# First plain tile closed early, and casts ahead of low parts where a gated MLP's blocks begin: a float32 trunk on one Trainium2 core

## The chip, the cores and the metric

The kernel runs on one core of one Trainium2 chip, as one program. The metric is the time of one execution on the device in microseconds (us). The times of before are the median of three runs, and one further execution was profiled. The engines are called as the profile calls them: PE is TensorE (PEld its weight loads), DVE is VectorE, ACT is ScalarE, POOL is GpSimd, and SP is SyncE, which only issues transfers here.

## The reference

A two-layer encoder trunk over 512 tokens of width 1024, in float32. Layer 0 mixes by a matrix memory (mLSTM), layer 1 by chunked band attention, and both read a memory of 256 tokens by cross attention. What matters here is the channel mixer that closes each layer:

```python
def causal_dwconv(x, w, b):              # width 3 here
    k = w.shape[0]
    ...
    y = xp[:, 0:s] * w[0]
    for j in range(1, k):
        y = y + xp[:, j:j + s] * w[j]
    return y + b

def conv_ffn(h, w_up, conv_w, conv_b, w_down):
    u, g = jnp.split(h @ w_up, 2, axis=-1)
    g = causal_dwconv(g, conv_w, conv_b)
    return (jax.nn.silu(g) * u) @ w_down

# in each layer l:
x = x + conv_ffn(rmsnorm(x, norm_ffn_g[l]), ffn_w_up[l], ffn_conv_w[l], ffn_conv_b[l], ffn_w_down[l])
```

The hidden width is 2816, so there are 22 tiles of 128 hidden channels.

## The kernel before

Activations lie with channels on the 128 partitions and the 512 tokens along the row. A float32 product is made of three matmuls. Each operand is split into a high part (ACT casts it, line 145, or line 900 for two tiles) and a low part (DVE subtracts the high part from the original, line 146 or 896); then high x high, high x low and low x high are added up in one bank (lines 201 to 203). So every weight that arrives costs a cast on ACT and then a subtraction on DVE. In names, `wr` is a raw weight as loaded, `wh`/`wl` are its parts, `fh`/`fl` those of a block or a block sum, and `u` holds the parts of activations and of hidden tiles.

The channel mixer works through the 22 hidden tiles in order. Tiles 0 and 1 are *plain*: one chain of 24 matmuls of 512 columns for the gate, one for the up projection (`plain_chain`). A plain tile goes on like this: the gate is scaled by the norm's row (line 787), gets its last tap and bias on ACT (line 770) and the other two taps on DVE (line 763), then a Silu on ACT, then the product with the up projection on DVE, and is split into parts (`keep`), which the down projection reads.

From tile 2 on (`PLAIN = 2`) a tile is a *block tile*: `step` makes the products of its gate and up weights with half as wide matmuls by a scheme with sums of blocks (seven block products instead of eight). The block sums of weights are DVE subtractions (line 1051), whose results are split like weights (`Forms`); the block sums of activations (line 807) are made once, by `block_sums`, whose parts are drawn one at a time by `forms(n)`. Within a step the bank `r1` serves several block products one after the other, and ACT copies it out each time (lines 972 and 983); bank `r3` goes to DVE (lines 1005 and 1109). Behind these products a step also issues the down projection's products of earlier hidden tiles (`down_products`), whose results ACT copies out (line 834) and POOL adds up in memory by DMA. `Tail` is what remains of a block tile, its scaling, taps, Silu and split; the next step does it.

PE, ACT and DVE execute in the order in which the code is written (`tc.manual_schedule(engines=ORDERED)`); no scheduler reorders them there. Each of these engines takes its instructions in that order, and semaphores make it wait for tiles of the others. Loads go through SP's queue, each as soon as its buffer is free.

High and low parts of weights have three pairs of buffers; `weight_tiles` gives out pairs 0, 1, 2 in turn or the one that is asked for. Down weights of the first block tiles use pair 2, like the second plain tile's up weights.

The mixer runs twice, in layer 0 (first block tile at about 296 us) and in layer 1 (at about 850 us).

Of the kernel before, what the change touches and what calls it, by code (L numbers as in the profile page):

```python
# [12 lines left out]
AF = mybir.ActivationFunctionType  # L13
ALU = mybir.AluOpType
# [28 lines left out]
PLAIN, LAST, LATE = 2, 6, 8  # L43
# [11 lines left out]
def f(ap):  # L55
    return ap.bitcast(F32)
# [3 lines left out]
def trunk(  # L60
# [19 lines left out]
    V, A, G = nc.vector, nc.scalar, nc.gpsimd  # L80
# [27 lines left out]
    def small(n=4, dtype=F32):  # L108
# [15 lines left out]
        out=maskf, in_=maskf, pattern=[[1, P]], base=0, channel_multiplier=-1,  # L124
# [28 lines left out]
    def load(src, a, b, extra=None):  # L153
        n = b + (extra.shape[-1] if extra is not None else 0)
        raw = sb("wr", [P, D])[:, : a * n].rearrange("p (a b) -> p a b", a=a)
        if isinstance(src, list):
            for i, one in enumerate(src):
                nc.sync.dma_start(raw[:, i, :], one)
        else:
            loads.append(nc.sync.dma_start(raw[:, :, :b], src))  # L160
        if extra is not None:
            nc.sync.dma_start(raw[:, :, b:], extra)
        return raw
# [3 lines left out]
    def weight_tiles(a, b, block=None):  # L167


        i = turn[0] % 3 if block is None else block  # L170
        turn[0] = i + 1
        tiles = []
        for tag in ("wh", "wl"):
            t = sb(f"{tag}{i}", [P, D + HALF * (i < 2)], F32R)


            at = HALF if i < 2 and (block is None) == (tag == "wh") else 0
            tiles.append(t[:, at : at + a * b].rearrange("p (a b) -> p a b", a=a))
        return tiles
# [15 lines left out]
    def rows(w, c0, n, k0=0, k1=None):  # L195
        k1 = k1 if k1 is not None else w.shape[0] // P
        return w[k0 * P : k1 * P, c0 : c0 + n].rearrange("(k p) c -> p k c", p=P)
# [18 lines left out]
    def run(gen):  # L216
        while True:
            try:
                next(gen)
            except StopIteration as end:  # L220
                return end.value
# [519 lines left out]
    class ChannelMixer:  # L741
# [146 lines left out]
        def tiles(self):  # L888
            norm, prep = self.norm, self.prep

            def forms(n):
                for _ in range(n):
                    next(self.forms, None)

            def split_low(w, raw):
                V.tensor_tensor(out=w[1], in0=raw, in1=f(w[0]), op=ALU.subtract)

            def split_high(raw, block=None):
                w = weight_tiles(*raw.shape[1:], block)
                A.copy(w[0], raw)  # L900
                return w

            def weights_load(j, up):
                return load(rows(self.w, j * P + (0 if up else DFF), P), KT, P)

            def own_sums():
                yield
                for part in prep.all_sums():
                    part()
                    yield  # L910

            turn[0] += (2 - turn[0]) % 3
            w = self.weights_of(0, False), self.weights_of(0, True)
            raw1, raw2 = weights_load(1, False), weights_load(1, True)
            prep.load_down()
            with tc.issue_after(loads[-1].ins):
                nxt = Forms(self, PLAIN + 1)
            first = self.forms if self.l else own_sums()
            with tc.manual_schedule(engines=ORDERED):
                og = run(self.plain_chain(0, False, w[0]))  # L920
                next(first)
                norm.halve()
                w1 = split_high(raw1)
                next(first)
                norm.total()
                next(first)
                split_low(w1, raw1)
                norm.logarithm()
                next(first)
                norm.power()  # L930
                forms(1)
                norm.refine()
                ou = run(self.plain_chain(0, True, w[1]))
                acc, taps = self.plain_gate(0, og)
                run(taps)
                w2 = split_high(raw2)
                forms(1)
                A.activation(acc, acc, AF.Silu)
                split_low(w2, raw2)
                forms(2)  # L940
                prep.split_up()
                og = run(self.plain_chain(1, False, w1))
                forms(1)
                acc1, taps = self.plain_gate(1, og)
                forms(1)
                run(taps)
                forms(2)
                run(self.forms)
                A.activation(acc1, acc1, AF.Silu)
                prep.split_second()  # L950
                prep.split_sums()
                V.tensor_tensor(out=acc, in0=ou, in1=acc, op=ALU.mult)
                ou = run(self.plain_chain(1, True, w2))
                tail, nxt = self.step(PLAIN, prep, nxt, None, (acc, acc1, ou))
                for j in range(PLAIN + 1, FT):
                    self.beside()
                    tail, nxt = self.step(j, nxt, Forms(self, j + 1) if j + 1 < FT else None, tail)
            for part in (
                tail.last_block, tail.scaled, tail.first_tap, tail.scaled_up,
                tail.second_tap, tail.third_tap, tail.silu, tail.gated, tail.split,  # L960
            ):
                part()

        def step(self, j, w, nxt, tail, plain=None):
            def then(o, *names):
                for name in names if o is not None else ():
                    getattr(o, name)()

            def sum_products(o, r, w, i):

                self.products(r, w, self.t(i))
                A.copy(o, r[:, :H])  # L972

            new = Tail(self, j)
            late = self.load_late(LATE_ROW[j]) if j in LATE_ROW else None
            then(tail, "last_block", "scaled")
            if tail is not None:
                w.split_fourth()
            then(tail, "scaled_up")
            r1, r2, new.r3 = ps("mm"), ps("mm"), ps("sc")  # L980
            new.up, new.u3, new.pre = sb("t", [P, S]), sb("t", [P, S]), sb("t", [P, S])
            self.products(r1, w.a11, self.b(0, 0), True)
            A.copy(new.up[:, :H], r1[:, :H])  # L983
            if tail is None:
                self.keep(plain[0])
                w.split_down()
                V.tensor_tensor(out=plain[1], in0=plain[2], in1=plain[1], op=ALU.mult)
            then(tail, "first_tap", "second_tap", "third_tap")
            self.products(r2, w.a12, self.b(1, 0), True)
            V.tensor_tensor(out=new.up[:, :H], in0=new.up[:, :H], in1=r2[:, :H], op=ALU.add)  # L990
            sum_products(new.up[:, H:], r1, w.s2, 2)
            if tail is None:
                self.keep(plain[1])
                w.split_gate()
                w.split_fourth()
            then(tail, "silu")
            first, rest = (None, nxt) if tail is None else (nxt, None)
            then(first, "sums")
            self.products(new.r3, w.s1, self.t(1), True)
            then(tail, "gated")  # L1000
            then(first, "split_second", "sum_third")
            sum_products(new.u3[:, :H], r1, w.s3, 3)
            then(tail, "split")
            then(first, "split_up")
            V.tensor_tensor(out=new.pre[:, H:], in0=new.u3[:, :H], in1=new.r3[:, :H], op=ALU.add)
            w.down_products(0, 2)
            then(first, "split_sums", "sum_fourth")
            w.add_down(0)
            then(first, "split_gate")
            w.add_down(1)  # L1010
            then(rest, "sums", "split_up", "split_second", "sum_third", "split_sums", "sum_fourth", "split_gate")
            then(first, "split_down")
            sum_products(new.pre[:, :H], r1, w.a22, 4)
            w.down_products(2, 4)
            self.products(new.r3, w.s4, self.b(1, 1))
            w.add_down(2)
            w.add_down(3)
            then(rest, "split_down")
            if late is not None:
                self.late_row(LATE_ROW[j], late)  # L1020
            return new, nxt
# [571 lines left out]
    sums = [[] for _ in range(TT)]  # L1593
# [109 lines left out]
```

## Time and profile before

| | us |
|---|---|
| median of 3 runs | 1178.28 (1178.22 to 1178.95) |
| profiled execution, its time | 1178.1 |
| its span | 1176.1 |
| PE busy | 1162.6 (99%) |
| PE weight loads busy | 1036.5 (88%) |
| DVE busy | 992.7 (84%) |
| ACT busy | 747.7 (64%) |
| granted clock of PE, mean | 0.998 |

Busy times are of one core over the span. A row of the timeline gives start, duration, engine, line, operation, tiles written and read, shape and count; in brackets stand the engine's idle time before it and what ended it. A matmul's duration covers its pipeline and overlaps the next one's, so the distance between starts tells the pace.

### The profile page before, as it was taken

The page shows a single profiled execution, that of the slowest core. Times are in us where ns is not written, and L with a number is a line of the kernel's source. Part 1 is how long each engine was busy: PE and PEld are TensorE (multiplying, and loading weights), DVE is VectorE, ACT ScalarE, POOL GpSimd, SP SyncE. Part 2 cuts the span into 40 slices and gives each one's busy share as a digit, 9 for nine tenths or more (in the row PEclk, how much of TensorE's full clock was granted, in tenths as well). Part 3 has the DMA queues.
Part 4 walks back from the last instruction along what each step waited for, and adds up shares of the span by engine and source line. Part 5 has one row for each costly group of instructions (what it writes and reads, how often), then busy time and mean ns, then how long its engine had stood idle before and what let it go on. Part 6 is the DMA issues. An engine that isn't in the chain of part 4 may idle for free.

```text
span 1176.1 us, 19341 instructions
## 1 busy us (share of the span) xinstructions
PE 1162.6 (99%) x7221; PEld 1036.5 (88%) x7221; DVE 992.7 (84%) x1776; ACT 747.7 (64%) x1347; POOL 151.2 (13%) x254
## 2 busy tenths in 40 slices
PE   9999999999999999999999999999999999999997
PEld 9988888888899999999888888778889999999986
DVE  6776788879899988888788888898989998888865
ACT  6548677657666655555676676776766765555545
POOL 1111101010121222111020000101010111111100
PEclk9999999999999999999999999999999999999999
DMA  8645325244468888876573313235345767777651
GB/s 285 223 112 146 80 55 152 67 153 125 126 162 187 203 185 199 190 167 141 153 218 104 90 57 106 92 92 178 113 138 148 154 150 176 178 179 171 134 162 72
DMA packets 204784, 171.27 MB, mean 146 GB/s; under 512 B 9256, under 2 KB 177934, under 8 KB 204690
## 3 DMA queue, kind: packets, MB, share of 16 engines
q1 hardware_dynamic: 184946, 123.93, 36.2%
q0 software_dynamic: 19168, 45.06, 19.4%
q8 instruction: 56, 0.92, 0.3%
q10 hardware_dynamic: 576, 1.05, 0.2%
q14 instruction: 38, 0.31, 0.1%
HBM read 133.09 MB, written 40.85 MB: 148 GB/s over the span
## 4 chain that ended last, share of the span: by engine, by line
PE 83%; DVE 10%; ACT 4%; issue 2%; DMA 1%; SPq 0%; POOL 0%; DVEq 0%; ACTq 0%; POOLq 0%
PE pmm L201 16%; PE pmm L202 16%; PE pmm L203 16%; PE ptr L202 6%; PE ptr L203 5%; PE ptr L201 5%; PE psc L201 4%; PE psc L202 4%; PE psc L203 4%; PE psc L620 2%; DVE wl L146 2%; PE ptr L1525 1%; ACT wh L145 1%; DVE t L807 1%; DVE u L146 1%
## 5 line engine op out<-in xcount | busy, mean ns | idle before, releaser
L201 PE MATMUL pmm<-u,wh 128*128 128x256 f32 (+1 forms) x992 | 334.9, 338 | 1.1 <-ACT t L972 0.9
L203 PE MATMUL pmm<-u,wl 128*128 128x256 f32 (+1 forms) x992 | 332.0, 335 | 0.0
L202 PE MATMUL pmm<-u,wh 128*128 128x256 f32 (+1 forms) x992 | 331.9, 335 | 0.0
L146 DVE TENSOR_TENSOR wl<-wr,wh 128x1024 fp32r<-128x1024 f32 (+4 forms) x166 | 186.1, 1121 | 68.6 <-ACT wh L145 68.2
L145 ACT CAST wh<-wr 128x1024 fp32r<-128x1024 f32 (+4 forms) x166 | 160.6, 970 | 67.9 <-PE pmm L202 30.1
L203 PEld LDWEIGHTS pmm<-u,wl 128*128 128x128 f32 x992 | 186.3, 188 | 18.9
L201 PEld LDWEIGHTS pmm<-u,wh 128*128 128x128 f32 x992 | 186.4, 188 | 18.0 <-ACT t L972 1.3
L202 PEld LDWEIGHTS pmm<-u,wh 128*128 128x128 f32 x992 | 186.5, 188 | 16.2 <-DVE u L146 0.5
L202 PE MATMUL ptr<-u,wh 128*128 128x512 f32 x272 | 106.5, 392 | 0.4 <-DVE u L146 0.4
L201 PE MATMUL ptr<-u,wh 128*128 128x512 f32 x272 | 106.7, 392 | 0.0
L203 PE MATMUL ptr<-u,wl 128*128 128x512 f32 x272 | 105.8, 389 | 0.0
L145 ACT CAST fh<-pt 128x512 fp32r<-128x512 f32 x120 | 74.7, 624 | 34.6 <-DVE pt L1051 33.5
L201 PE MATMUL pmm<-u,fh 128*128 128x256 f32 x320 | 89.0, 278 | 0.2 <-ACT t L983 0.2
L202 PE MATMUL pmm<-u,fh 128*128 128x256 f32 x320 | 88.6, 277 | 0.0
L203 PE MATMUL pmm<-u,fl 128*128 128x256 f32 x320 | 88.4, 276 | 0.0
L972 ACT COPY t<-pmm 128x256 f32<-128x256 f32 x120 | 44.9, 374 | 64.4 <-PE pmm L203 64.3
L146 DVE TENSOR_TENSOR fl<-pt,fh 128x512 fp32r<-128x512 f32 x120 | 82.2, 687 | 3.2
L763 DVE SCALAR_TENSOR_TENSOR t<-t,cols,t 128x511 f32<-128x511 f32 x88 | 65.9, 749 | 10.0 <-ACT t L770 8.5
L201 PE MATMUL psc<-u,wh 128*128 128x256 f32 (+1 forms) x208 | 63.2, 304 | 0.0
L203 PE MATMUL psc<-u,wl 128*128 128x256 f32 (+1 forms) x208 | 63.0, 303 | 0.0
L202 PE MATMUL psc<-u,wh 128*128 128x256 f32 (+1 forms) x208 | 63.0, 303 | 0.0
L201 PEld LDWEIGHTS pmm<-u,fh 128*128 128x128 f32 x320 | 60.1, 188 | 2.8 <-ACT t L972 0.7
(360 smaller groups left out, 2637.0 us busy)
## 6 DMA issues: line engine op xcount, KB each, us to landing
wr<-in_ffn_w_up_dram SPq DMA_DIRECT2D x46, 512.0 KB, 8.5
pt<-in_ffn_w_up_dram SPq DMA_DIRECT2D x40, 512.0 KB, 8.1
wr<-in_ffn_w_down_dram SPq DMA_DIRECT2D x32, 512.0 KB, 5.2
wr<-in_a_w_in_dram SPq DMA_DIRECT2D x20, 512.0 KB, 3.9
xspill<-bias POOLq DMA_DIRECT2D x32, 256.0 KB, 7.0
without_row<-bias POOLq DMA_DIRECT2D x24, 256.0 KB, 4.1
wr<-in_w_kv_dram SPq DMA_DIRECT2D x12, 512.0 KB, 3.9
without_row<-t POOLq DMA_DIRECT2D x24, 256.0 KB, 4.2
```

The costliest lines, as they stand in the source:

```text
L145: high = A.copy(hi, src) if on_act else V.tensor_copy(hi, src)
L146: low = V.tensor_tensor(out=lo, in0=src, in1=f(hi), op=ALU.subtract)
L201: nc.tensor.matmul(o, lh, rh, start=first, stop=False, skip_group_check=more)
L202: nc.tensor.matmul(o, lh, rl, start=False, stop=False, skip_group_check=more)
L203: nc.tensor.matmul(o, ll, rh, start=False, stop=last, skip_group_check=more)
L620: nc.tensor.matmul(o, a, b, start=first and i == 0, stop=i == 1)
L763: V.scalar_tensor_tensor(acc[:, n:], src[:, : S - n], self.fw[:, c * FT + j : c * FT + j + 1], acc[:, n:], op0=ALU.mult, op1=ALU.add,)
L807: V.tensor_tensor(out=o, in0=x, in1=y, op=ALU.subtract)
L972: A.copy(o, r[:, :H])
L1525: nc.tensor.transpose(tp[:, b * P : (b + 1) * P], es[T, h][:, b * P : (b + 1) * P], ident)
```

## The change

The change rewrites the order in which ACT and DVE get their work between the first plain tile and the second block tile. PE's, POOL's and SP's orders stay as they are. In `tiles`, the first plain tile's product with its up projection and its split (`keep`) move up behind its Silu. They stood behind the second tile's Silu and in the first step. The second plain tile's product moves up too, to stand before the first step, and the first step's down weights are split there. Parts of the block sums of activations (`forms`) now stand before the taps. In `step`, the first block tile's third weight sum and the cast of up weights for the next one come earlier, ahead of the copies of down products, and the next tile's down weights are split inside the next step.

```diff
                 acc, taps = self.plain_gate(0, og)
+                forms(1)
                 run(taps)
+                forms(2)
                 w2 = split_high(raw2)
-                forms(1)
+                split_low(w2, raw2)
                 A.activation(acc, acc, AF.Silu)
-                split_low(w2, raw2)
-                forms(2)
+                V.tensor_tensor(out=acc, in0=ou, in1=acc, op=ALU.mult)
                 prep.split_up()
                 og = run(self.plain_chain(1, False, w1))
                 forms(1)
+                self.keep(acc)
                 acc1, taps = self.plain_gate(1, og)
                 forms(1)
                 run(taps)
                 forms(2)
                 run(self.forms)
-                A.activation(acc1, acc1, AF.Silu)
                 prep.split_second()
                 prep.split_sums()
-                V.tensor_tensor(out=acc, in0=ou, in1=acc, op=ALU.mult)
+                A.activation(acc1, acc1, AF.Silu)
                 ou = run(self.plain_chain(1, True, w2))
-                tail, nxt = self.step(PLAIN, prep, nxt, None, (acc, acc1, ou))
+                V.tensor_tensor(out=acc1, in0=ou, in1=acc1, op=ALU.mult)
+                prep.split_down()
+                tail, nxt = self.step(PLAIN, prep, nxt, None, acc1)
...
             A.copy(new.up[:, :H], r1[:, :H])
             if tail is None:
-                self.keep(plain[0])
+                self.keep(plain)
+            if j == PLAIN + 1:
                 w.split_down()
-                V.tensor_tensor(out=plain[1], in0=plain[2], in1=plain[1], op=ALU.mult)
...
             sum_products(new.up[:, H:], r1, w.s2, 2)
             if tail is None:
-                self.keep(plain[1])
                 w.split_gate()
                 w.split_fourth()
...
             then(first, "split_sums", "sum_fourth")
+            then(rest, "sums", "sum_third", "split_up")
             w.add_down(0)
             then(first, "split_gate")
             w.add_down(1)
-            then(rest, "sums", "split_up", "split_second", "sum_third", "split_sums", "sum_fourth", "split_gate")
+            then(rest, "split_second", "split_sums", "sum_fourth", "split_gate")
             then(first, "split_down")
...
             w.add_down(3)
-            then(rest, "split_down")
             if late is not None:
```

Three places show what this does to the engines' orders, in layer 0; layer 1 has the same.

First, ACT where the first block tile (step 2) begins. `t_3100` and `t_3160` (after: `t_3165`) are the gates of plain tiles 0 and 1, `pmm_3215` (after: `pmm_3224`) is the bank `r1`, `wr_3012` the down weights of step 2. Before:

```order
L949 ACTIVATE t_3160<-t_3160 128x512
L145 CAST fh_3181<-pt_2792 128x512
L145 CAST wh_3185<-pt_2792 128x1024
L983 COPY t_3218<-pmm_3215 128x256
L145 CAST u_3234<-t_3100 128x512
L145 CAST wh_3238<-wr_3012 128x1024
L972 COPY t_3218<-pmm_3215 128x256
L145 CAST u_3269<-t_3160 128x512
```

And after:

```order
L145 CAST fh_3185<-pt_2792 128x512
L145 CAST wh_3189<-pt_2792 128x1024
L953 ACTIVATE t_3165<-t_3165 128x512
L145 CAST wh_3220<-wr_3012 128x1024
L986 COPY t_3227<-pmm_3224 128x256
L145 CAST u_3243<-t_3165 128x512
L975 COPY t_3227<-pmm_3224 128x256
```

The cast of the down weights moved ahead of the first copy of the bank. Between the two copies stands one cast instead of two, the second plain tile's, which used to follow the second copy; the first plain tile's cast has gone to an earlier place.

Second, DVE from the first plain tile's taps on (line 763), up to the second tile's scaling by the norm's row (line 787). `wr_3010` is the second plain tile's up weight, `psc_3075` the first tile's up projection. Before:

```order
L763 SCALAR_TENSOR_TENSOR t_3100<-t_3101,cols_799,t_3100 128x511
L763 SCALAR_TENSOR_TENSOR t_3100<-t_3101,cols_799,t_3100 128x510
L807 TENSOR_TENSOR t_3109<-u_3068 128x256
L807 TENSOR_TENSOR t_3109<-u_3069,t_3109 128x256
L807 TENSOR_TENSOR t_3110<-u_3069,u_3068 128x256
L807 TENSOR_TENSOR t_3110<-u_3069,t_3109 128x256
L896 TENSOR_TENSOR wl_3107<-wr_3010,wh_3106 128x1024
L146 TENSOR_TENSOR u_3118<-t_3109,u_3117 128x512
L146 TENSOR_TENSOR u_3122<-t_3110,u_3121 128x512
L146 TENSOR_TENSOR wl_3126<-pt_2791,wh_3125 128x512
L146 TENSOR_TENSOR wl_3126<-pt_2792,wh_3125 128x512
L787 TENSOR_TENSOR t_3161<-pmm_3131,rb_3073 128x512
```

And after, from the first pair of differences' second half on:

```order
L807 TENSOR_TENSOR t_3105<-u_3069,t_3104 128x256
L763 SCALAR_TENSOR_TENSOR t_3100<-t_3101,cols_799,t_3100 128x511
L763 SCALAR_TENSOR_TENSOR t_3100<-t_3101,cols_799,t_3100 128x510
L146 TENSOR_TENSOR u_3113<-t_3104,u_3112 128x512
L146 TENSOR_TENSOR u_3117<-t_3105,u_3116 128x512
L896 TENSOR_TENSOR wl_3121<-wr_3010,wh_3120 128x1024
L941 TENSOR_TENSOR t_3100<-psc_3075,t_3100 128x512
L146 TENSOR_TENSOR wl_3127<-pt_2791,wh_3126 128x512
L146 TENSOR_TENSOR wl_3127<-pt_2792,wh_3126 128x512
L146 TENSOR_TENSOR u_3162<-t_3100,u_3161 128x512
L787 TENSOR_TENSOR t_3166<-pmm_3132,rb_3073 128x512
```

The four differences (line 807) moved ahead of the taps, the low part of `wr_3010` moved behind the low parts of the sums, and the first tile's product and low part came in before line 787.

Third, DVE at the end of step 2, from the first weight sums for step 3 (line 1051, after: 1053) to the first addition of its tail (line 1109, after: 1111). `wr_3015` holds step 3's up weights, `wr_3017` its down weights. Before:

```order
L1051 TENSOR_TENSOR pt_2792<-pt_2792,wr_3015 128x512
L146 TENSOR_TENSOR wl_3330<-wr_3015,wh_3329 128x1024
L146 TENSOR_TENSOR fl_3334<-pt_2792,fh_3333 128x512
L1051 TENSOR_TENSOR pt_2792<-wr_3015,pt_2791 128x512
L146 TENSOR_TENSOR wl_3339<-pt_2792,wh_3338 128x1024
L1051 TENSOR_TENSOR pt_2792<-wr_3015,pt_2792 128x512
L146 TENSOR_TENSOR fl_3344<-pt_2791,fh_3343 128x512
L146 TENSOR_TENSOR wl_3393<-wr_3017,wh_3392 128x512
L1109 TENSOR_TENSOR t_3218<-t_3218,psc_3217 128x256
```

And after:

```order
L1053 TENSOR_TENSOR pt_2792<-pt_2792,wr_3015 128x512
L1053 TENSOR_TENSOR pt_2792<-wr_3015,pt_2791 128x512
L146 TENSOR_TENSOR wl_3325<-wr_3015,wh_3324 128x1024
L146 TENSOR_TENSOR fl_3335<-pt_2792,fh_3334 128x512
L146 TENSOR_TENSOR wl_3339<-pt_2792,wh_3338 128x1024
L1053 TENSOR_TENSOR pt_2792<-wr_3015,pt_2792 128x512
L146 TENSOR_TENSOR fl_3344<-pt_2791,fh_3343 128x512
L1111 TENSOR_TENSOR t_3227<-t_3227,psc_3226 128x256
```

The third sum moved ahead of the low parts, and the low part of the down weights went behind line 1111, into step 3.

## The prediction

> **What bounds the kernel now.** I read the page first, then the windows around the two first block tiles, then TensorE's own rows in order of time, and last the rows of ScalarE and VectorE in front of each gap. The page gives the span and the busy shares.
>
> ```profile
> span 1176.1 us, 19341 instructions
> PE 1162.6 (99%) x7221; PEld 1036.5 (88%) x7221; DVE 992.7 (84%) x1776; ACT 747.7 (64%) x1347; POOL 151.2 (13%) x254
> ```
>
> TensorE (PE) is the bound, and whatever changes the time must change its idle time: 1176.1 - 1162.6 = 13.5 us. The windows show what the steps just behind the changed ones look like, in layer 0 and layer 1 (columns: us, then busy us and count of each engine, granted clock, DMA share, GB/s).
>
> ```profile
> 326.00:338.00 12.00, 12.00 (x93) 11.51 (x92) 11.31 (x19) 8.15 (x15) 1.80 (x4) 1.00 0.67 170
> 880.00:892.00 12.00, 12.00 (x93) 11.51 (x92) 11.30 (x19) 8.04 (x15) 0.66 (x3) 1.00 0.49 143
> ```
>
> There PE is full at clock 1.00 while VectorE (DVE) has 0.7 us of 12 left. So time that PE wins ahead of these stretches should arrive at the end. Now PE's starts around the first block tile (step 2) and the next (step 3), layer 0 and then layer 1. In brackets stand idle time and who ended it.
>
> ```profile
> 290.33 0.39 PE L201 MATMUL psc<-u,wh 128*128 128x512 f32 x1
> ...
> 301.18 0.28 PE L203 MATMUL psc<-u,wl 128*128 128x256 f32 x1
> 301.90 0.38 PE L201 MATMUL pmm<-u,wh 128*128 128x256 f32 x1 [0.45 <-ACT t L972]
> 302.12 0.28 PE L202 MATMUL pmm<-u,wh 128*128 128x256 f32 x1
> ...
> 303.60 0.40 PE L202 MATMUL ptr<-u,wh 128*128 128x512 f32 x1
> 303.84 0.39 PE L203 MATMUL ptr<-u,wl 128*128 128x512 f32 x1
> 304.15 0.50 PE L201 MATMUL ptr<-u,wh 128*128 128x512 f32 x1
> 304.87 0.50 PE L202 MATMUL ptr<-u,wh 128*128 128x512 f32 x1 [0.22 <-DVE u L146]
> ...
> 314.90 0.28 PE L203 MATMUL pmm<-u,wl 128*128 128x256 f32 x1
> 315.27 0.39 PE L201 MATMUL pmm<-u,fh 128*128 128x256 f32 x1
> ...
> 323.68 0.28 PE L203 MATMUL pmm<-u,fl 128*128 128x256 f32 x1
> 324.39 0.39 PE L201 MATMUL psc<-u,fh 128*128 128x256 f32 x1 [0.44 <-DVE t L1005]
> ...
> 854.98 0.28 PE L203 MATMUL psc<-u,wl 128*128 128x256 f32 x1
> 855.73 0.38 PE L201 MATMUL pmm<-u,wh 128*128 128x256 f32 x1 [0.47 <-ACT t L972]
> ...
> 877.26 0.28 PE L202 MATMUL pmm<-u,fh 128*128 128x256 f32 x1
> 877.37 0.28 PE L203 MATMUL pmm<-u,fl 128*128 128x256 f32 x1
> 878.55 0.39 PE L201 MATMUL psc<-u,fh 128*128 128x256 f32 x1 [0.91 <-DVE t L1005]
> ```
>
> Undisturbed, 256-column matmuls start 0.11 us apart (877.26, 877.37) and 512-column ones 0.23 to 0.24 (303.60, 303.84). I measure gaps between starts against that, since the idle time in brackets ends at a modelled end: at 301.90 it says 0.45, the starts say 0.72 - 0.11 = 0.61, and the restarted matmul then costs 0.11 more (302.12 comes 0.22 later, not 0.11). With 0.11 for each restart, layer 0 loses 0.72 at 301.90; 0.72 - 0.23 + 0.11 = 0.60 at 304.87 and 0.08 one matmul earlier, so 0.68; 0.37 at 315.27 and 0.71 at 324.39: together 2.48. Layer 1 loses 0.75 at 855.73 and 1.18 at 878.55; for its other two I take layer 0's 0.68 and 0.37, an estimate, so 2.98. These 5.46 us are all that the change can win. [...]
>
> **The change part by part.** PE, GpSimd and SyncE keep their order; the same instructions are issued, with the same shapes. What follows moves work within ScalarE (ACT) and VectorE.
>
> First tile, ACT and DVE up to the second tile's taps. The rows of before that I build on:
>
> ```profile
> 285.76 1.54 DVE L763 SCALAR_TENSOR_TENSOR t<-t,cols,t 128x511 f32<-128x511 f32 x2 [0.88 <-ACT t L770]
> 288.68 1.21 DVE L896 TENSOR_TENSOR wl<-wr,wh 128x1024 fp32r<-128x1024 f32 x1
> 294.40 1.53 DVE L763 SCALAR_TENSOR_TENSOR t<-t,cols,t 128x511 f32<-128x511 f32 x2
> 299.30 0.68 DVE L952 TENSOR_TENSOR t<-psc,t 128x512 f32<-128x512 f32 x1
> 300.67 0.69 DVE L146 TENSOR_TENSOR u<-t,u 128x512 fp32r<-128x512 f32 x1 [0.69 <-ACT u L145]
> ```
>
> Successive instructions overlap by 0.08 on DVE and 0.09 on ACT, so an idle stretch loses that much more than it shows. The four differences of a block sum now stand before the first tile's taps and fill DVE's wait of 0.88, worth 0.96. Against that the first tile's product (0.68 less the overlap, 0.60), its low part (0.60) and that part's wait for its cast (0.69 at 300.67, worth 0.77) now come before the second tile's taps. Net 0.60 + 0.60 + 0.77 - 0.96 = 1.0 us later: the taps run from 295.4 to 296.9 instead of 294.40 to 295.93. The low part of the second up weights (288.68, ending 289.89) gets two low parts more ahead of it (2 x 0.60) and the wait less (0.96): it lands 0.24 later, at about 290.13. PE's chain starts at 290.33 and uses low weights in its third matmul, 0.45 later, so 0.6 us remain.
>
> Now ACT at the first block product:
>
> ```profile
> 296.03 0.63 ACT L949 ACTIVATE t<-t 128x512 f32<-128x512 f32 x1 [0.89 <-DVE t L763]
> 296.56 0.60 ACT L145 CAST fh<-pt 128x512 fp32r<-128x512 f32 x1
> 297.07 1.04 ACT L145 CAST wh<-pt 128x1024 fp32r<-128x1024 f32 x1
> 298.03 0.36 ACT L983 COPY t<-pmm 128x256 f32<-128x256 f32 x1
> 300.01 0.62 ACT L145 CAST u<-t 128x512 fp32r<-128x512 f32 x1 [1.63 <-DVE t L952]
> 300.54 1.04 ACT L145 CAST wh<-wr 128x1024 fp32r<-128x1024 f32 x1
> 303.47 0.62 ACT L145 CAST u<-t 128x512 fp32r<-128x512 f32 x1 [1.62 <-DVE t L987]
> ```
>
> Before, ACT went idle at 296.03 - 0.89 = 295.14, behind the casts of the block sum; with DVE 1.0 us later it gets there at about 296.05. Now the two casts for the block run first (0.51 + 0.96, to 297.5), while the taps end; then the Silu (0.53, to 298.05), and then, new at this place, the cast of the down weights (0.95, to 299.0). Only then comes the copy that empties the bank of the first product, ending at 299.35; before it ended at 298.39. PE wants that bank at 298.50 (twenty-four products at 0.11 behind the chain's end at 295.77). So a new stall of 0.85 plus the restart's 0.10: 0.95 us in each layer. This is the one cost that I see. Nothing is loaded late for that cast: the same weights were cast at 300.54.
>
> What it pays. The wait at 301.90: its copy stood behind the cast at 300.01, which waited 1.63 us for the product on DVE, and behind the 1.04 us cast. In the new order the copy has one short cast ahead, and DVE makes that cast's input (second product) right after the low parts of the sums, at about 300 to 300.7. The copy then starts when its products end, 298.50 + 0.95 + 1.4 = 300.85 or a little later, and has 1.4 us (the twelve products of the next bank) before PE needs it. 0.72 and 0.75 go. The wait at 304.87: the second tile's low part needed the cast at 303.47, which waited 1.62 for its product on DVE; now the product ends at 300.7 and the low part, behind that of the down weights (1.22), at 302.5, while PE asks for it not before 304. 0.68 in each layer goes.
>
> The end of step 2, DVE:
>
> ```profile
> 308.58 1.22 DVE L146 TENSOR_TENSOR wl<-wr,wh 128x1024 fp32r<-128x1024 f32 x1 [0.91 <-ACT wh L145]
> 312.18 1.23 DVE L146 TENSOR_TENSOR wl<-pt,wh 128x1024 fp32r<-128x1024 f32 x1 [1.17 <-ACT wh L145]
> ```
>
> Both waits of a low part for its cast go. The third sum (0.60) now stands ahead of the first low part, the cast of the up weights stands ahead of ACT's two copies of down products, and the second cast no longer waits for the third sum. DVE gains 0.91 + 1.17 = 2.08 us before step 3. The step's down weights (cast 0.52, low part 0.60) move from here into step 3, so ACT's copy at 315.27 has one cast less ahead, and the 0.37 goes. At 324.39 and 878.55 PE waits for a DVE addition that is 0.60 and 1.07 us late. PE itself comes 0.72 + 0.68 + 0.37 - 0.95 = 0.82 us earlier, so DVE must be 1.42 and 1.89 us faster; it has 2.08. 0.71 and 1.18 go, in layer 1 by a margin of only 0.2. The low part moved into step 3 is asked for by the down products some 3 us later, and it frees its raw buffer at most a few tenths otherwise than now, so the next load by SyncE is not pressed.
>
> The sum: -5.46 + 2 x 0.95 = -3.56 us. The profiled execution took 1178.1 us (span 1176.1 and 2.0 around it): 1174.5. The median of the runs, 1178.28, lies 0.18 above it, so I forecast 1174.7 for the median. Without any new stall it is 1172.8. If the new stall is twice as long, 1176.6. Both ends are near in the trace: no stall is what the copy at 298.03 shows now, and twice is one more cast of 0.95.
>
> **The rivals.** (a) The last stall stays: DVE is still late at 324.39 and 878.55, because it does not collect its 2.08 us (if it waits for PE's last product of step 2 instead). For it speaks the thin margin in layer 1; against it that DVE waits there only for ACT. 0.71 + 1.18 come back: 1176.6.
>
> (b) The table load. It now follows busy ACT directly, where before ACT had idled. If the engine drained first, Silu and all behind it would be up to one load later. The row nearest to that:
>
> ```profile
> 173.71 1.28 ACT L1288 ACT_TABLE_LOAD   x1
> 175.00 0.63 ACT L1288 ACTIVATE t<-t 128x512 f32<-128x512 f32 x1
> ...
> 287.38 1.28 ACT L938 ACT_TABLE_LOAD   x1 [0.70 <-DVE t L763]
> ```
>
> At 173.71 the load follows an instruction without idle time, and the next starts 0.01 us after its end, so I expect 1.28 flat. A delay of another 1.28 would reach the copy in full: 2 x 1.28 = 2.56, so 1177.3. [...]
>
> (c) DVE is the real bound behind step 3 (11.31 of 12 busy) and PE's lead is used up there: 1178.3, no change. Against it PE has no gap in 12 us.
>
> (d) Slower: the second up weights' low part. Its place behind taps and low parts leaves 0.6 us. If DVE comes there x us later, PE's chain at 290.33 stalls x - 0.6 in each layer. At x = 2.4 the gain of 3.56 is gone (2 x 1.8), and from there it decides; at x = 3.7 the time is 1174.7 + 2 x 3.1 = 1180.9. It would need taps or casts that run that late, and nothing ahead of them has moved but what is counted here.
>
> **How the numbers follow.** The forecast's mechanism gets 0.72, with 1172.8 to 1176.6 as its own range; (a) 0.09, (b) 0.05, (c) 0.08, (d) 0.06. About 0.2% (2.4 us) is what a measurement can tell from no change, so faster means below 1175.9. A little of the first case ends above that, and (a), (b), (c) count as the same: faster 0.71, same 0.23, slower 0.06. The range takes in the first case and (a): 1172.9 to 1176.8.
>
> **What would show it.** In the changed trace: no PE wait for the copy at L975 near 302, none for a low part at L146 near 304.5, none for the addition at L1007; one wait of 0.5 to 1.0 us for the copy at L986 about 299.3 and 853; DVE without waits for casts near 306 to 310. Most likely wrong are the new stall's size, by what ACT loses ahead of it, and the last stall of layer 1.

## The result, and the profile after

The changed kernel took 1174.48 us (median of 7 runs, 1174.03 to 1175.14) beside 1178.27 us for the kernel before (7 runs, 1177.93 to 1178.95): a ratio of 0.9967 with a 95% interval from 0.9956 to 0.9979, so 3.8 us less. The forecast was 1174.7, with a range from 1172.9 to 1176.8. The profiled execution of the changed kernel took 1174.31 us. First its page: span and busy times.

```profile
span 1172.3 us, 19341 instructions
PE 1160.6 (99%) x7221; PEld 1036.6 (88%) x7221; DVE 992.8 (85%) x1776; ACT 748.8 (64%) x1347; POOL 151.7 (13%) x254
```

DVE, ACT and POOL have the busy time that they had to within 1.1 us, so no work was saved there; 3.8 us went out of the span. The view of the waits of PE over the whole span (who waits for whom, us in total, times, longest) begins like this:

```profile
PE pmm L201 <- ACT t L986: 1.5, 2, 0.8
PE pmm L490 <- DVE mcf L132: 1.1, 1, 1.1
PE psc L620 <- DVE s L1512: 0.3, 1, 0.3
```

The waits for L975 (before: L972), for the low part at L146 and for L1007 (before: L1005) are no longer in it, and the one wait that the prediction adds, for the copy at L986, is, once in each layer. PE's rows there, layer 0 and layer 1:

```profile
299.02 0.28 PE L203 MATMUL pmm<-u,wl 128*128 128x256 f32 x1
300.08 0.39 PE L201 MATMUL pmm<-u,fh 128*128 128x256 f32 x1 [0.78 <-ACT t L986]
300.30 0.28 PE L202 MATMUL pmm<-u,fh 128*128 128x256 f32 x1
...
850.71 0.28 PE L203 MATMUL pmm<-u,wl 128*128 128x256 f32 x1
851.75 0.39 PE L201 MATMUL pmm<-u,fh 128*128 128x256 f32 x1 [0.76 <-ACT t L986]
```

Measured by starts as in the prediction, the stall is 300.08 - 299.02 - 0.11 = 0.95 and 0.11 more at the restart (300.30): 1.06 us, and 1.04 in layer 1. It is the only gap of PE left in the two stretches. Adding up every late start there gives 2.53 + 3.04 = 5.57 us lost before and 1.05 + 1.04 = 2.09 after: 3.48 us won, where the prediction had 3.56.

ACT ahead of that copy, from the table load on:

```profile
285.55 0.82 ACT L770 ACTIVATE t<-t,cols 128x512 f32<-128x512 f32 x1 [1.99 <-DVE t L787]
...
288.67 1.28 ACT L940 ACT_TABLE_LOAD   x1
289.96 0.63 ACT L940 ACTIVATE t<-t 128x512 f32<-128x512 f32 x1
...
298.19 0.63 ACT L953 ACTIVATE t<-t 128x512 f32<-128x512 f32 x1
298.73 1.03 ACT L145 CAST wh<-wr 128x1024 fp32r<-128x1024 f32 x1
299.66 0.36 ACT L986 COPY t<-pmm 128x256 f32<-128x256 f32 x1
301.19 0.62 ACT L145 CAST u<-t 128x512 fp32r<-128x512 f32 x1 [1.16 <-DVE t L955]
301.80 0.38 ACT L975 COPY t<-pmm 128x256 f32<-128x256 f32 x1
```

The row at 285.55 stands ahead of everything that the change moved, and it stood at 284.92 before: this profile is 0.63 us later there already, by its start alone. Take that off, and the copy ends at 300.02 - 0.63 = 299.39, where 299.35 was forecast. The copy at 301.80 now has one short cast ahead of it and is in time. DVE:

```profile
289.62 1.22 DVE L896 TENSOR_TENSOR wl<-wr,wh 128x1024 fp32r<-128x1024 f32 x1
...
296.08 1.53 DVE L763 SCALAR_TENSOR_TENSOR t<-t,cols,t 128x511 f32<-128x511 f32 x2
...
309.48 1.23 DVE L146 TENSOR_TENSOR wl<-pt,wh 128x1024 fp32r<-128x1024 f32 x1 [0.25 <-ACT wh L145]
...
874.40 0.41 DVE L1007 TENSOR_TENSOR t<-t,psc 128x256 f32<-128x256 f32 x1
```

The low part of the second up weights ends at 290.84, 290.21 without the 0.63 (forecast 290.13), the taps begin at 295.45 (forecast 295.4). Of the two waits for casts at the end of step 2, 0.91 and 1.17, one of 0.25 is left. The addition at 874.40 ends at 874.81, and PE's matmul that waited for it before starts at 875.28, without a wait.

### The profile page after: what moved, and what is told of

Read it like the earlier page. It is cut to its first block, busy times and chain, and to the rows that moved or that the text cites. A ratio compares the mean times of both kernels' runs of the same rounds, so it can differ in the third digit from the quotient of the medians.

```text
span 1172.3 us, 19341 instructions
## 1 busy us (share of the span) xinstructions
PE 1160.6 (99%) x7221; PEld 1036.6 (88%) x7221; DVE 992.8 (85%) x1776; ACT 748.8 (64%) x1347; POOL 151.7 (13%) x254
## 3 DMA queue, kind: packets, MB, share of 16 engines
q10 hardware_dynamic: 576, 1.05, 0.2%
## 4 chain that ended last, share of the span: by engine, by line
PE 88%; DVE 6%; ACT 4%; issue 1%; DMA 1%; SPq 0%; POOL 0%; DVEq 0%; ACTq 0%; POOLq 0%
PE pmm L201 17%; PE pmm L202 16%; PE pmm L203 16%; PE ptr L202 6%; PE ptr L201 6%; PE ptr L203 6%; PE psc L202 4%; PE psc L203 4%; PE psc L201 4%; PE psc L620 2%; PE ptr L1527 1%; DVE t L807 1%; DVE rb L296 1%; ACT wh L145 1%; PE ptr L1548 1%
## 5 line engine op out<-in xcount | busy, mean ns | idle before, releaser
L146 DVE TENSOR_TENSOR wl<-wr,wh 128x1024 fp32r<-128x1024 f32 (+4 forms) x166 | 186.2, 1122 | 67.2 <-ACT wh L145 66.7
L975 ACT COPY t<-pmm 128x256 f32<-128x256 f32 x120 | 45.1, 376 | 69.3 <-PE pmm L203 69.2
L146 DVE TENSOR_TENSOR fl<-pt,fh 128x512 fp32r<-128x512 f32 x120 | 82.3, 688 | 3.0
```

Of the source, the lines that this page charges most:

```text
L146: low = V.tensor_tensor(out=lo, in0=src, in1=f(hi), op=ALU.subtract)
```

## The experiments

Each kernel was timed in five rounds beside the kernel before on the same chip. Those of one group share a chip and the runs of before.

**First group (before: 1178.53 us, 15 runs).** The changed kernel with the cast of the first block tile's down weights put behind the copy of the first bank:

```diff
-                prep.split_down()
                 tail, nxt = self.step(PLAIN, prep, nxt, None, acc1)
...
             A.copy(new.up[:, :H], r1[:, :H])
+            if tail is None or j == PLAIN + 1:
+                w.split_down()
             if tail is None:
                 self.keep(plain)
-            if j == PLAIN + 1:
-                w.split_down()
```

> The changed kernel with one edit: the down weights of the first block tile are cast behind the first copy of bank r1, not ahead of it. My theory (PE's stalls at the block tiles add up to the time): the one stall that the change made, 1.05 us in layer 0 and 1.04 in layer 1, goes; 1174.48 - 2.1 = 1172.4 us, and PE has no gap between 284 and 335 us. Rival (VectorE is the real limit behind the block tiles, PE's lead is used up there): a gap comes back later in steps 3 to 5 and the time stays at 1174.5. Second rival (the cast is needed early, for the down products): a new PE wait for a low part L146 near 304, up to 1 us in each layer, 1173.5 to 1174.5.

It took 1172.55 us (1172.32 to 1173.02), ratio 0.995 (0.9938 to 0.9963). ACT and PE at that place:

```profile
298.40 0.62 ACT L953 ACTIVATE t<-t 128x512 f32<-128x512 f32 x1
298.93 0.35 ACT L985 COPY t<-pmm 128x256 f32<-128x256 f32 x1
299.18 1.05 ACT L145 CAST wh<-wr 128x1024 fp32r<-128x1024 f32 x1
```

```profile
299.20 0.28 PE L203 MATMUL pmm<-u,wl 128*128 128x256 f32 x1
299.33 0.39 PE L201 MATMUL pmm<-u,fh 128*128 128x256 f32 x1
299.56 0.28 PE L202 MATMUL pmm<-u,fh 128*128 128x256 f32 x1
```

The copy starts as its products end and the stall is gone but for a restart of 0.11. The cast that stood ahead of the copy was the whole stall, and its 2 us in two layers arrive at the end. This version is the fastest of the three: its ratio to the kernel before is 0.995, the changed kernel's, on another chip, 0.9967.

The part of the change that lies around the plain tiles alone (the changed kernel with the end of the step and the next tile's down weights as before):

```diff
-            if j == PLAIN + 1:
-                w.split_down()
...
-            then(rest, "sums", "sum_third", "split_up")
             w.add_down(0)
...
-            then(rest, "split_second", "split_sums", "sum_fourth", "split_gate")
+            then(rest, "sums", "split_up", "split_second", "sum_third", "split_sums", "sum_fourth", "split_gate")
...
             w.add_down(3)
+            then(rest, "split_down")
```

> Only the part of the change in the plain tiles (first tile closed early, sums ahead of the taps, down weights of step 2 cast before the step); step 2's end in the order of before. My theory: the waits at 301.90 and 304.87 go (0.72 + 0.68 and 0.75 + 0.69), the new stall comes (1.05 and 1.04), the two waits of step 3 stay (0.37 + 0.71 and 0.43 + 1.18): 1178.27 - 2.84 + 2.09 = 1177.5 us. PE waits for the copy at L986, and then for L1005's addition as before. Rival (the plain tiles' part carries the change): 1175 us or less. Rival (PE's lead only turns into a longer wait at step 3, since VectorE's arrival there is set by its own casts): 1178.3.

1177.32 us (1176.62 to 1179.08, 11 runs), ratio 0.9993 (0.9984 to 1.0002). The complement, the kernel before with that end of the step and nothing else:

> Only the part in the step (third sum and the up weights' cast earlier at the end of step 2, step 3's down weights split inside step 3); the plain tiles in the order of before. My theory: the two waits of step 3 go (0.37 + 0.71 and 0.43 + 1.18 = 2.69), the waits at 301.90 and 304.87 stay and no new stall comes: 1178.27 - 2.69 = 1175.6 us. Rival (the plain tiles' part carries the change): 1178. Rival (both parts are needed together): 1177 to 1178.

1174.33 us (1174.12 to 1175.22), ratio 0.9964 (0.995 to 0.9977). PE's rows, of the first kernel and then of the second:

```profile
315.22 0.39 PE L201 MATMUL pmm<-u,fh 128*128 128x256 f32 x1
324.34 0.39 PE L201 MATMUL psc<-u,fh 128*128 128x256 f32 x1 [0.45 <-DVE t L1005]
```

```profile
302.60 0.39 PE L201 MATMUL pmm<-u,wh 128*128 128x256 f32 x1 [0.45 <-ACT t L972]
305.57 0.51 PE L202 MATMUL ptr<-u,wh 128*128 128x512 f32 x1 [0.22 <-DVE u L146]
```

Each part takes away its own two stalls, as forecast: the plain tiles' part those near 302 and 305, and it alone brings the new one; the step's part those near 315 and 324. But the step's part came out 1.3 us better than expected. The starts give 1.38 + 1.24 = 2.62 us lost, 2.95 less than before, while the time is 4.2 us less. Some 0.7 us of the rest is a matter of PE's pace, below, and the remainder isn't explained; the interval of the ratio reaches from 2.7 to 5.9 us.

The changed kernel with the next tile's down weights split at the end of the step, where they were:

```diff
-            if j == PLAIN + 1:
-                w.split_down()
...
             w.add_down(3)
+            then(rest, "split_down")
```

> The changed kernel with one edit undone: step 3's down weights are split at the end of step 2 again. My forecast gave the wait at 315.27 (0.37 and 0.43) to this move, because ScalarE has one cast less ahead of the copy. By that the two waits come back: 1174.48 + 0.8 = 1175.3 us, with a PE wait for L986 near 315. Rival: ScalarE has 1.6 us idle ahead of that copy in the changed kernel and VectorE 0.96 us ahead of the addition at L1111, so one cast and one low part more cost nothing: 1174.5 and no PE wait there.

1173.78 us (1173.55 to 1175.53), ratio 0.9963 (0.995 to 0.9975): no loss, so the rival holds. The copy that PE waited for at 315.27, first in the kernel before, then in this one (ACT):

```profile
311.10 1.05 ACT L145 CAST wh<-pt 128x1024 fp32r<-128x1024 f32 x1 [2.03 <-DVE pt L1051]
...
314.83 0.39 ACT L983 COPY t<-pmm 128x256 f32<-128x256 f32 x1
```

```profile
308.11 1.05 ACT L145 CAST wh<-pt 128x1024 fp32r<-128x1024 f32 x1
...
311.71 0.62 ACT L145 CAST wh<-wr 128x512 fp32r<-128x512 f32 x1
312.23 0.62 ACT L145 CAST fh<-pt 128x512 fp32r<-128x512 f32 x1
313.95 0.37 ACT L986 COPY t<-pmm 128x256 f32<-128x256 f32 x1 [1.10 <-PE pmm L203]
```

With the third sum and the cast of the up weights early, the cast at 311.10 (here 308.11) no longer waits 2.03 us for DVE, and ACT has 1.10 us to spare at the copy with the cast of the down weights still ahead of it. No run moves the third sum without the other cast, so what each of the two gives is not shown.

**Second group (before: 1178.08 us, 16 runs).** The fourth rival's place: the version with the cast behind the copy, and the low part of the second up weights late.

```diff
                 w2 = split_high(raw2)
-                split_low(w2, raw2)
                 A.activation(acc, acc, AF.Silu)
                 V.tensor_tensor(out=acc, in0=ou, in1=acc, op=ALU.mult)
                 prep.split_up()
+                split_low(w2, raw2)
```

> The version with the cast behind the copy, and one thing more: the low part of the second up weights goes to VectorE behind the first tile's product and behind the low parts of the first block's up weights, instead of ahead of them. It tests the fourth rival's place and whether time that TensorE loses there reaches the end. My theory: TensorE is the bound and each stall arrives in full. In the version that it starts from (1172.55 us) the Silu on ScalarE ends at 290.79, so the product runs to about 291.5, two low parts to 292.7, and the weights' low part to 293.8; TensorE's chain starts at 291.15 and asks for those weights 0.45 later, at 291.60. So a stall of 2.2 and 0.1 for the restart, in each of two layers: 1177.2. Rival: VectorE bounds the stretch behind and TensorE's lead there is worth nothing, so the time stays at 1172.6; a rival in between, where half of the loss is made up behind it: 1174.9.

> The version with the cast behind the copy once more, as the base of the two that start from it, on the same chip: 1172.5, with no wait of TensorE between the two chains of the first block tile. Rival, if its first result was luck: 1174.5, like the changed kernel.

The base took 1172.91 us (1172.18 to 1172.93), ratio 0.9954 (0.9942 to 0.9967), again without the wait. With the low part late it took 1178.04 us (1175.79 to 1179.99, 11 runs), ratio 0.9996 (0.9987 to 1.0004): 5.1 us more, 0.5 above my theory. PE in layer 0 and layer 1, and then PE's granted clock behind the second stall (the last three numbers are the clock, the DMA share and GB/s):

```profile
291.20 0.39 PE L202 MATMUL psc<-u,wh 128*128 128x512 f32 x1
293.73 0.50 PE L203 MATMUL psc<-u,wl 128*128 128x512 f32 x1 [2.14 <-DVE wl L896]
...
844.09 0.39 PE L202 MATMUL psc<-u,wh 128*128 128x512 f32 x1
846.58 0.80 PE L203 MATMUL psc<-u,wl 128*128 128x512 f32 x1 [2.10 <-DVE wl L896]
847.18 0.63 PE L201 MATMUL psc<-u,wh 128*128 128x512 f32 x1
847.60 0.63 PE L202 MATMUL psc<-u,wh 128*128 128x512 f32 x1
```

```profile
846.40:850.20 3.80, 3.62 (x9) 2.90 (x10) 3.73 (x9) 2.38 (x4) 0.00 (x0) 0.55 0.23 69
```

The stalls are 293.73 - 291.20 - 0.23 = 2.30 and 846.58 - 844.09 - 0.23 = 2.26, as forecast (2.2). Behind the second the matmuls start 0.42 apart, not 0.23, at a granted clock of 0.55. So a longer stall can cost twice, in this execution in one layer of two: 2.41 in layer 0, 3.90 in layer 1. The 11 runs spread from 1175.79 to 1179.99, and only this one was profiled, so in how many of them the clock fell, and in which layer, is not shown.

The changed kernel with the forms around the first tile's taps as before:

```diff
-                forms(1)
                 run(taps)
-                forms(2)
                 w2 = split_high(raw2)
-                split_low(w2, raw2)
+                forms(1)
                 A.activation(acc, acc, AF.Silu)
+                split_low(w2, raw2)
+                forms(2)
                 V.tensor_tensor(out=acc, in0=ou, in1=acc, op=ALU.mult)
```

> The changed kernel with the order around the first tile's taps as before (the differences of the block sum behind the taps, their casts and low parts behind the Silu), and the product where the change put it. It tests whether the new stall at the copy is set by the chain of ScalarE and VectorE work ahead of it. My theory: ScalarE, busy without a break from 286.41 to 293.37 in the changed kernel, idles ahead of the table load again (0.70 shown before the change, 0.79 with the overlap), and everything behind it up to the copy is that much later, so the stall grows from 1.05 to 1.84 us in each layer: 1174.5 + 1.6 = 1176.1. Rival: some slack on the way (VectorE's wait of 0.77 at 293.41, ScalarE's of 1.36 at 294.74) takes it up: 1174.5.

1174.45 us (1174.17 to 1174.85, 6 runs), ratio 0.997 (0.9958 to 0.9982). The stall does grow, but only by half of what I expected:

```profile
298.32 0.28 PE L203 MATMUL pmm<-u,wl 128*128 128x256 f32 x1
299.76 0.39 PE L201 MATMUL pmm<-u,fh 128*128 128x256 f32 x1 [1.17 <-ACT t L986]
```

That is 1.33 and 0.11, so 1.44 for 1.05, and 1.40 in layer 1. My error was to count ACT's new idle time of 0.79 in full. In the changed kernel the two casts ahead of the table load wait a little for DVE's differences, and the load starts 3.12 us behind the row of L770 (285.55, 288.67). Here it starts 2.46 behind it, and the two casts take 1.03 behind the Silu: 3.49, only 0.37 more. The time doesn't show even these 0.7 us, but the 1174.48 beside it is from another chip; both kernels on one chip stand below.

The version with the cast behind the copy and the next tile's split at the end of the step:

> The version with the cast behind the copy, and the next tile's down weights split at the end of the first block tile's step as before the change. It asks whether the 0.7 us by which the changed kernel with that split put back lay lower (1173.78 against 1174.48) is real. My theory: the trace shows the same stalls of TensorE in both, so the difference is scatter and this version takes what the one with the cast behind the copy takes: 1172.5. Rival: the earlier split is worth 0.6 us by itself: 1171.9.

1172.57 us (1172.19 to 1173.14), ratio 0.9953 (0.994 to 0.9965). That is 0.3 us from the base, within the scatter of its runs: no effect of the place of that split can be seen, and the 0.7 us were scatter.

**Third group (before: 1178.33 us, 22 runs).** Known doses: the cast of the down weights ahead of the copy done once, twice and three times.

```diff
-    def split(hi, lo, src, on_act=True, pinned=False):
+    def split(hi, lo, src, on_act=True, pinned=False, again=0):
+        for _ in range(again):
+            A.copy(hi, src)
         high = A.copy(hi, src) if on_act else V.tensor_copy(hi, src)
...
-                prep.split_down()
+                prep.split_down(1)
```

`split_down` hands the number on to `split`; three casts are `split_down(2)`.

> The changed kernel as it is, once more, on the chip on which the doses are run: 1174.5, with a stall of 1.05 us in each layer. It is the base of the doses and of the kernel with the forms as before.

> The changed kernel with the cast of the first block tile's down weights done twice, one directly behind the other, ahead of the copy that empties the first bank. A known dose: 0.95 us more of ScalarE in each layer, with the new stall at 1.05 us now. My theory: the stall becomes 2.0 us and arrives in full, 1174.5 + 1.9 = 1176.4. Rival: the stretch behind makes the time up, 1174.5. Second rival: behind a stall of 2 us TensorE's granted clock falls, as it did to 0.55 for 3.8 us behind the stall of 2.3 us in layer 1 of the kernel with the late low part, which cost 1.5 us there and nothing in layer 0: 1176.4 to 1179.4.

> The same with the cast done three times: 1.9 us more of ScalarE in each layer. My theory: a stall of 2.95 us in each layer, 1174.5 + 3.8 = 1178.3, if the granted clock stays at 1.00. Rival: the clock falls to about 0.55 for 3 to 4 us behind each stall of this length, 1.5 us more for each layer where it does: 1179.8 to 1181.3.

> The changed kernel with the order around the first tile's taps as before, once more, beside the changed kernel. In its first profile the stall was 1.44 and 1.39 us in place of 1.05, but its time was the changed kernel's (1174.45 against 1174.48), and its profile shows 1.1 us less lost by TensorE in the first 20 us. My theory: the stalls count and the start is scatter, so it comes out 0.7 us above the changed kernel of this group, 1175.2. Rival: something else pays it back each time, 1174.5.

| ahead of the copy | lost at PE, layer 0 and 1 | time, us | ratio |
|---|---|---|---|
| nothing (the base of group 2) | 0.27, 0.36 | 1172.91 (1172.18 to 1172.93) | 0.9954 (0.9942 to 0.9967) |
| one cast (the changed kernel) | 1.05, 1.02 | 1174.03 (1173.44 to 1174.81) | 0.9963 (0.995 to 0.9975) |
| one cast, forms as before | 1.45, 1.40 | 1175.03 (1174.0 to 1175.28) | 0.997 (0.9959 to 0.9982) |
| two casts | 2.13, 2.11 | 1176.39 (1175.5 to 1178.86) | 0.9987 (0.9978 to 0.9996) |
| three casts | 4.81, 3.17 | 1181.03 (1179.9 to 1183.5) | 1.0021 (1.0012 to 1.003) |

From one cast to two PE loses 2.17 us more and the time grows by 2.36; the forms as before lose 0.78 more and cost 1.00. Nothing behind the stall pays it back. In the second group the profile of the forms as before had started 0.70 earlier than that of the changed kernel (284.85 and 285.55 at the row of L770), which hid as much in its span. The stall with two casts is 2.13 and not 2.0 because the second cast of the same tile starts 1.06 behind the first (298.06, 299.12). With three casts (its lines stand two lower in the code) PE and the clock in layer 0:

```profile
298.47 0.28 PE L205 MATMUL pmm<-u,wl 128*128 128x256 f32 x1
301.69 0.39 PE L203 MATMUL pmm<-u,fh 128*128 128x256 f32 x1 [2.94 <-ACT t L988]
...
303.05 0.41 PE L203 MATMUL pmm<-u,fh 128*128 128x256 f32 x1
303.26 0.41 PE L204 MATMUL pmm<-u,fh 128*128 128x256 f32 x1
```

```profile
301.70:306.00 4.30, 4.30 (x23) 4.30 (x24) 3.00 (x5) 1.87 (x4) 0.00 (x0) 0.61 0.46 125
```

Here the stall is 3.11, and soon behind the restart matmuls start 0.21 apart, not 0.11. That makes 4.81 in layer 0; in layer 1 the clock stayed at 1.00 and 3.17 were lost. So the rival with the falling clock holds for this dose in one layer of two, and the gain is turned into a loss. The profiled execution took 1179.9 us, the least of the 11 runs; whether the others lost twice in both layers is not shown. Two casts showed no fall in the profiled execution, which was again the fastest of its runs. One of the 11 took 1178.86 us at a mean granted clock of 0.995, where the others had 0.997 to 0.999; that would fit a fall, but it was not profiled.

## Why the prediction was right, and where its terms were off

**The stalls that go.** All four of each layer went, and the two halves of the change each took away the two that the prediction gave to it. The sum of them was 5.46 with two entries taken over from layer 0; measured in both layers it was 5.57.

**The new stall.** Forecast 0.95 in each layer, measured 1.06 and 1.04. ACT's copy ended within 0.04 us of the forecast. The term is 0.1 too small because of that 0.04 and because PE restarts 0.06 behind the copy's end (300.02, 300.08), which the working left out. The kernel without that cast and the doses show that the cast is the cause and that its price reaches the end.

**The wrong step.** The prediction said that the 0.37 at 315.27 goes because the next tile's down weights leave the step. The kernel with that split put back shows otherwise: the 0.37 stays away without that move. By the trace it goes because the third sum comes ahead of the low parts and of their waits, so that ACT's next cast no longer waits 2.03 us for DVE. The move of the down weights is worth nothing that the runs show, with the new stall or without it.

**The margins.** At the last stall the prediction left DVE 2.08 - 1.42 = 0.66 us in layer 0 and 0.2 in layer 1. The trace has the same in both: 323.59 - 323.12 = 0.47 and 875.28 - 874.81 = 0.47. So the stall went, but not by the sum of 2.08. DVE is 1.5 us ahead already when it begins the sums at the end of step 2 (305.40 against 306.27, and the later start of 0.63), which was in no term; in the kernel with the plain tiles' part alone that lead is lost in a wait of 2.18 us for the cast of the up weights (0.91 before). In the changed kernel DVE waits 0.25 for a cast and then, behind the low parts, 0.96 for PE's last product of step 2, in layer 1 as in layer 0:

```profile
312.88 0.42 DVE L1111 TENSOR_TENSOR t<-t,psc 128x256 f32<-128x256 f32 x1 [0.96 <-PE psc L203]
```

That is the wait on which the first rival was to rest; the prediction held against it that DVE waits there only for ACT, as it does in the kernel before. The stall stays away all the same: DVE's work from that wait to its addition ends 0.47 before PE asks for it.

**The other rivals.** The table load took 1.28 flat, 0.02 behind a cast of ACT that ends at 288.65, and the Silu started 0.01 behind its end (288.67, then 289.96; in layer 1 840.34, then 841.63). So the second rival falls: no row shows the further 1.28 that it set down. The third, that DVE takes PE's lead back, falls by the doses, which count about one for one. The fourth has about the price that it was given, 5.1 us where stalls of 2.3 in each layer make 4.6: a low part that came 2.3 us too late for PE took all that the best version had won.

**What the working left out.** The prediction called 326 to 338 and 880 to 892 full by PE's busy 12.00. The same windows in the changed kernel:

```profile
326.00:338.00 12.00, 12.00 (x96) 11.51 (x95) 11.40 (x19) 8.44 (x15) 2.22 (x4) 1.00 0.63 172
880.00:892.00 12.00, 12.00 (x96) 11.51 (x96) 11.40 (x19) 8.43 (x15) 1.08 (x2) 1.00 0.47 146
```

Busy is 12.00 again, but with 96 matmuls where there were 93. Two pairs of rows, fifteen matmuls apart each, first of before and then of after:

```profile
328.05 0.28 PE L201 MATMUL pmm<-u,wh 128*128 128x256 f32 x1
329.84 0.28 PE L201 MATMUL pmm<-u,fh 128*128 128x256 f32 x1
```

```profile
328.01 0.28 PE L201 MATMUL pmm<-u,fh 128*128 128x256 f32 x1
329.71 0.28 PE L201 MATMUL psc<-u,wh 128*128 128x256 f32 x1
```

Before, they start 0.119 apart, after, 0.113. With equal matmuls of the two traces set beside each other, the changed kernel's distance goes from +0.63 at 280 us to -1.30 at 333 (1.93 won in layer 0, of which the stalls explain 1.48), stands at -1.55 at 837 and reaches -3.77 at 887 (2.22, stalls 2.00). So some 0.7 us of the gain came from pace, and 0.25 arose between the layers; neither was in a term. The later start of this profile, 0.63, hid most of that. That the total met the forecast within 0.2 us is partly this luck.

## What to carry to other kernels

Where PE is the bound, list its lost starts one by one, find for each the instruction that it waits for, and then ask what an order puts newly ahead of each short copy that empties a bank: a cast of 0.95 us that nobody awaits yet, moved ahead of a copy of 0.35 us that PE awaits, cost 1 us in each layer, and behind the copy it was free. Split a change into its halves, and move each piece by itself: of this one, one piece was a cost and another did nothing that could be measured. Measure a busy stretch by the number of instructions in it, since PE's busy share can stay full when its pace is lower (12.00 us of 12 here, with 93 matmuls as with 96).

## What the runs showed of the hardware that I had not expected

**A slower pace behind some restarts.** Behind the stalls at 315.27 and 324.39 in the kernel before, and behind the one at 300.08 in the changed one, matmuls of 256 columns started 0.118 to 0.120 us apart in place of 0.113, at a granted clock of 1.00, until the next 512-column products came (324.6 to 333 us before). Behind the stall of 0.72 at 301.90 in the kernel before, and behind that of 2.03 with two casts, they kept 0.113. And of two stalls of 0.95 us at the same place of layer 0, those at 300.08 in the changed kernel's first profile and at 299.81 in its profile of the third group, only the first had it: behind the second they kept 0.113 up to 303.99. So the length of the stall doesn't decide. What causes it stays open; no run here was made for it.

**The clock behind longer stalls.** Stalls of about 1 and 2 us left the granted clock at 1.00 in the profiles (changed kernel and two casts, both layers). One of two stalls of 2.3 us and one of two of 3.1 us came with a stretch of about 3.4 us at half the pace (0.42 for 0.23, 0.21 for 0.11; a mean of 0.55 over 3.80 us is 3.4 us at one half), which cost 1.5 to 1.6 us. With three casts the rows from 302.62 to 306.04 stand at that pace, 3.42 us. The other stall of each pair came with no such stretch. What decides between the two no run shows.

**The start.** Profiles of kernels that are equal up to there differ at the first plain tile: the row of L770 stands at 284.92 before, at 285.55 after, and between 284.65 and 285.74 in all fourteen profiles (two lines lower in the code with two and three casts). So a difference of less than 1.1 us (285.74 - 284.65) between the spans of two of these profiles means nothing before the start is taken off.
